# Last four gate tiles chunk by chunk, and the last unit's product, casts and loads rearranged, in a two-layer decoder step

## The chip, the cores and the metric

The kernel runs on one core of one Trainium2 chip. The metric is the device time of one execution in microseconds. Of the kernel before the change three runs are given: 1866.89 us in the median, 1864.61 to 1870.77 us.

## What is computed

One inference step of a decoder trunk of two layers on 1032 rows (1024 of a prompt and 8 samples), 1024 wide, inner width 2048, all in float32. Layer A is an HGRN2 recurrence; layer B is a chunked gated MLP. Behind each mixer comes the per-layer embedding, and at the end a norm. What matters here is the end of layer B:

```python
proj = h @ w_in                      # layer B: u, v, z
u, v, z = jnp.split(proj, 3, axis=-1)
u = jax.nn.gelu(u); v = layernorm(jax.nn.gelu(v), ln_g, ln_b)
s = jnp.einsum('gts,bnsgd->bntgd', w, vc) + b_sp.T[None, None, :, :, None]
y = (u * s * jax.nn.silu(z)) @ w_out
h = h + y
gate = jax.nn.sigmoid(rmsnorm(h, norm_ple[i]) @ w_ple_gate[i])
h = h + gate * (p[i] @ w_ple_proj[i])
return rmsnorm(h, norm_final), ...
```

## The kernel before, in words

**Layout.** Activations lie feature by row: 1032 columns (the rows of the model) in three chunks c0, c1 and c2 of 384, 384 and 264 columns (`CH`, widths `W`, offsets `OFF`), eight tiles of 128 features each. The residual is `hr[c][m]`. A float32 product is made of three TensorE matmuls (`mm3`, lines 228 to 230): both sides are split into a high part, which ScalarE casts, and a low part, which VectorE subtracts (`split`, `split_weights` at lines 149 and 150, `load_list` at 379 and 383), and the matmuls are high by high, high by low, low by high.

**Order.** TensorE's order is written out by hand: a main program, with side programs that are advanced at its ticks. The other engines' orders are made by a scheduler when the kernel is built, by dependencies and priorities (`high_priority`); on the chip each engine runs its own list in order. All the loads and stores around the change are issued by SyncE, in one order, over eight semaphore lanes: a transfer is issued once the one eight before it has landed.

**The last unit of layer B** (g = 7, lines 1580 to 1603). `unit` multiplies two feature tiles by two chunks with seven instead of eight block products, whose sums VectorE forms from the results in PSUM (`u`, `c`); one copy is on ScalarE (`u2`, line 493). In its turns `spatial` makes for each of two tiles and three chunks the product `psp` with the spatial weights (TensorE, 1526), adds the bias (VectorE, 1529), multiplies by u (GpSimd, 1535), and then by the sigmoid and by z (ScalarE 1541, VectorE 1542 and 1543), and stores the rows to `ozd` (1544). Hooks of this unit reload rows of `ozd` that the output projection needs, split them into the operands `xm[..]` and `hh/hl` (`load_zt`, `load_list`), and split p (`p_in_act`, in `first`) for p's products.

**The output projection** (`out_phase`, key "ob"). Its `begin` (1608 to 1626) starts the reload of the rows (2,0), which are chunk 2's first eight tiles (`load_zt(zt, [(2, 0)], ..., 1, 8)`: the first eight loads are issued, the splits follow later in `run(more)`), issues the loads of sums into the `hr` tiles (`load_sums`, line 1320: `h<-d3t`), and makes the second half of p's products (`pple`: `ps_pple` in PSUM, copied by ScalarE at 350 into eight tiles that are free here and, for chunk 2, into `hr[2]`, stored to `ppd` at 351). Behind them stands the first plain product, `ps_o`, for c0, c1 and c2 in turn: c0 reads `bh_12427`, c1 reads `xm[1]` for its first four tiles and `xm[0]` for its last four, c2 reads the rows (2,0), which are `hh[2]/hl[2]` (`bh_12429/bl_12432`). `xm[0]` is `xmh_10550/xml_10551`.

**The gates and the end** (`ple(1, ...)`). Gate tiles m = 0..7 each make 24 matmuls for a chunk, a sigmoid (1273), the product with `pj` (1274), the addition to `hr` (1275) and the squares (263, 264). Tiles 0 and 1, and 6 and 7, go in a pair, chunk by chunk; behind tile 7 of a chunk its final norm (`final`: 279, 282, 237, 290) and its outputs `yt` (1651 on GpSimd, 1653 on VectorE) and their stores (1655) follow.

Of the kernel before, what the change touches and what calls it, by code (L numbers as in the profile page):

```python
# [13 lines left out]
ALU = mybir.AluOpType  # L14
# [66 lines left out]
def trunk_kernel(ctx, tc, xT, st, pT, nrm, wina, lbl, gna, wouta, winb, lng, lnb, lngr, lnbr,  # L81
# [74 lines left out]
    staged = {}  # L156

# [7 lines left out]
    def load(n, wait=False):  # L165
        if n >= len(order) or n in loaded or wait and order[n][0] == "B":
            return
        if order[n][0][0].isupper():
            loaded[n] = load_unit(*order[n])
            return  # L170
        if n not in staged:
            fetch_weights(n)
        stg = staged.pop(n)
        with tc.high_priority(offset=PRI if order[n][:2] == ("p", 1) or order[n][0] in ("b", "g") else 0):
            loaded[n] = split_weights(stg, 1024, PLAIN, wp)
# [216 lines left out]
    def one(tile):  # L392
        return lambda w: tile()[:, :w].rearrange("p (k t) -> p k t", k=1)
# [873 lines left out]
    def ple(l, ep, hh, hl, ssq, done, mid=None):  # L1267
# [15 lines left out]
        def start(m):  # L1283
            pj = ep.tile([P, T], F32, name="pj", bufs=2)
            nc.sync.dma_start(pj, ppd[l][m])
            return take("g", l, m), pj

        def pair(m):
            a, b = start(m), start(m + 1)
            for c in CH:  # L1290
                group(m, c, *a)
                group(m + 1, c, *b)
                if m == KT - 2:
                    done(c)

        pair(0)
        for m in range(2, KT - 2):
            if m == 3 and mid:
                mid()
            a = start(m)  # L1300
            for c in CH:
                group(m, c, *a)
        pair(KT - 2)
# [208 lines left out]
    def spatial(g, vn, us, wt, then={}, early=False):  # L1512
# [8 lines left out]
        def pre(mm, c):  # L1521
# [13 lines left out]
            G.tensor_tensor(s[:, :w], s[:, :w], us[mm, c][:, :w], ALU.mult)  # L1535
# [25 lines left out]
    for g in range(8):  # L1561
# [18 lines left out]
        else:  # L1580
# [9 lines left out]
            zq = load_zt(zt, [(1, 0), (0, 0), (1, 4)],  # L1590
# [3 lines left out]
            def fetch(n):  # L1594
                return lambda: [next(zq, None) for _ in range(n)]

            def first():
                fetch(ZQ)()
                p_in_act(1, lambda w: ws[0].tile([P, 512], F32, name="ssum", bufs=2)[:, :w])

            spatial(g, vn, us, take("B", 2 * MI + 2 * g), {0: first, 1: lambda: next(sums), 2: fetch(4), 3: fetch(8), 4: fetch(4)}, True)
# [5 lines left out]
    def begin(up, raw, rows, load_h):  # L1607
# [10 lines left out]
        more = load_zt(zt, [(2, 0)], one(lambda: next(turns)()), 1, 8)  # L1618
# [11 lines left out]

    with ExitStack() as sE:
# [112 lines left out]
```

## Time and profile before

| what | us |
|---|---|
| median of three runs | 1866.89 (1864.61 to 1870.77) |
| the profiled execution, its own time | 1863.58 |
| its span, first to last instruction | 1861.6 |
| TensorE busy in the span | 1822.4 (98%) |
| VectorE busy | 1360.5 (73%) |
| ScalarE busy | 897.6 (48%) |
| GpSimd busy | 402.3 (22%) |
| granted TensorE clock, mean | 0.995 of full speed |

Times below are microseconds from the start of the span. An instruction's row gives its start, its duration, engine, line, operation, output and inputs with their tile names, and in brackets how long the engine had been idle and what released it. A row that is marked x4 holds four instructions in a run. In a table of windows stand the busy time of each engine and its number of instructions, the clock, the share of the 16 DMA engines and the bytes per second. The last unit runs from about 1545 to 1569, p's products from 1569 to 1583, the first `ps_o` from 1583 to 1594, and the gates fill the last 90 us.

### The profile page before, as it was taken

The numbers are of one execution on the slowest core, as the hardware profiler recorded it, in microseconds if no ns is written. First come the engines' busy times: TensorE is split into PE (matmuls) and PEld (weight loads), VectorE is DVE, ScalarE is ACT, GpSimd is POOL, SyncE is SP. The second block draws the span as 40 slices with busy tenths as digits, with TensorE's granted clock in tenths as the row PEclk, the third lists the DMA queues.
The fourth block names the chain that finished last, engine by engine and source line by source line (L and its number), as shares of the span: only waits on it lengthen the run. The fifth ranks groups of instructions, "written<-read, shape, count | busy, mean of one in ns | idle before, by whom it ended". The sixth has DMA issues, their size and how long they took to land.

```text
span 1861.6 us, 37133 instructions
## 1 busy us (share of the span) xinstructions
PE 1822.4 (98%) x14458; PEld 1788.6 (96%) x14458; DVE 1360.5 (73%) x2760; ACT 897.6 (48%) x1905; POOL 402.3 (22%) x407
## 2 busy tenths in 40 slices
PE   8999999999999999999999999999999999999997
PEld 7999999999999998999999999999999999999997
DVE  7766888889888875867756755577778877877744
ACT  7533366556656655344444544434443435444342
POOL 4000011111111110000323233354444552000222
PEclk9999999999999999999999999999999999999999
DMA  6233344345444355853244343323334546953223
GB/s 220 79 112 106 112 127 128 108 152 182 149 130 140 117 176 185 278 184 96 87 145 140 101 136 92 95 79 119 129 117 143 172 129 215 305 179 104 72 92 114
DMA packets 164560, 258.11 MB, mean 139 GB/s; under 512 B 16096, under 2 KB 136864, under 8 KB 163360
## 3 DMA queue, kind: packets, MB, share of 16 engines
q1 hardware_dynamic: 164384, 255.74, 43.5%
q8 instruction: 113, 1.85, 0.4%
q14 instruction: 63, 0.52, 0.1%
HBM read 182.88 MB, written 72.80 MB: 137 GB/s over the span
## 4 chain that ended last, share of the span: by engine, by line
PE 80%; DVE 10%; DMA 5%; issue 2%; POOL 1%; ACT 1%; SPq 0%; DVEq 0%; ACTq 0%; POOLq 0%
PE ps_proj L228 19%; PE ps_proj L230 18%; PE ps_proj L229 18%; PE ps_d L228 2%; PE ps_o L228 2%; PE ps_d L230 2%; PE ps_d L229 2%; PE ps_o L229 2%; PE ps_o L230 2%; DVE wlo L150 1%; PE psp L1526 1%; DMA vb<-vd 1%; PE pt_o L899 1%; PE pt_g L1408 1%; PE pC L807 1%
## 5 line engine op out<-in xcount | busy, mean ns | idle before, releaser
L228 PE MATMUL ps_proj<-bh,whi 128*128 128x264 f32 (+1 forms) x2248 | 719.2, 320 | 4.3 <-ACT u L493 1.3
L229 PE MATMUL ps_proj<-bl,whi 128*128 128x264 f32 (+1 forms) x2248 | 700.8, 312 | 5.4 <-DVE bl L224 2.7
L230 PE MATMUL ps_proj<-bh,wlo 128*128 128x264 f32 (+1 forms) x2248 | 700.9, 312 | 1.2 <-DVE wlo L150 1.2
L228 PEld LDWEIGHTS ps_proj<-bh,whi 128*128 128x128 f32 x2248 | 423.6, 188 | 12.3 <-issue 3.3
L229 PEld LDWEIGHTS ps_proj<-bl,whi 128*128 128x128 f32 x2248 | 424.1, 189 | 8.9 <-DVE bl L224 5.4
L230 PEld LDWEIGHTS ps_proj<-bh,wlo 128*128 128x128 f32 x2248 | 422.6, 188 | 2.1 <-DVE wlo L150 2.1
L150 DVE TENSOR_TENSOR wlo<-wstg,whi 128x1024 fp32r<-128x1024 f32 x148 | 183.7, 1241 | 109.4 <-ACT whi L149 109.1
L149 ACT CAST whi<-wstg 128x1024 fp32r<-128x1024 f32 x148 | 155.2, 1049 | 150.0 <-PE ps_proj L229 125.0
L149 ACT CAST shi<-ssum 128x512 fp32r<-128x512 f32 x152 | 94.1, 621 | 187.3 <-PE ps_proj L229 90.1
L150 DVE TENSOR_TENSOR slo<-ssum,shi 128x512 fp32r<-128x512 f32 x152 | 113.9, 751 | 9.2 <-ACT shi L149 8.8
L237 POOL TENSOR_TENSOR rsq<-rms_e,mhalf 128x3 f32<-128x3 f32 x15 | 17.8, 1187 | 368.1 <-DVE rms_e L282 368.1
L857 DVE TENSOR_TENSOR qk<-qk,t 128x384 f32<-128x384 f32 (+1 forms) x144 | 77.2, 540 | 12.0 <-PE pC L807 11.3
L228 PE MATMUL ps_proj<-xmh,shi 128*128 128x384 f32 x244 | 83.0, 340 | 1.9 <-ACT xmh L223 1.7
L229 PE MATMUL ps_proj<-xml,shi 128*128 128x384 f32 x244 | 81.9, 336 | 0.7 <-DVE xml L224 0.7
L230 PE MATMUL ps_proj<-xmh,slo 128*128 128x384 f32 x244 | 81.7, 335 | 0.0
L228 PE MATMUL ps_o<-bh,whi 128*128 128x384 f32 (+1 forms) x232 | 73.4, 316 | 0.0
L230 PE MATMUL ps_o<-bh,wlo 128*128 128x384 f32 (+1 forms) x232 | 72.7, 313 | 0.0
L229 PE MATMUL ps_o<-bl,whi 128*128 128x384 f32 (+1 forms) x232 | 72.7, 313 | 0.0
L1535 POOL TENSOR_TENSOR s<-s,u 128x384 f32<-128x384 f32 (+1 forms) x48 | 54.1, 1127 | 70.9 <-DVE s L1529 70.3
L1274 DVE TENSOR_TENSOR tmp<-tmp,pj 128x384 f32<-128x384 f32 (+1 forms) x48 | 25.6, 534 | 55.9 <-ACT tmp L1273 52.0
L237 POOL TENSOR_TENSOR rsq<-ss_e,mhalf 128x3 f32<-128x3 f32 (+2 forms) x32 | 28.4, 889 | 145.7 <-DVE ss_e L893 145.7
L264 POOL TENSOR_TENSOR ssq<-ssq,tmp 128x384 f32<-128x384 f32 (+1 forms) x36 | 34.3, 951 | 108.1 <-ACT tmp L263 108.1
(376 smaller groups left out, 4135.8 us busy)
## 6 DMA issues: line engine op xcount, KB each, us to landing
wstg<-in_wina SPq DMA_DIRECT2D x48, 512.0 KB, 3.8
wstg<-in_winb SPq DMA_DIRECT2D x48, 512.0 KB, 4.0
pj<-ppd SPq DMA_DIRECT2D x16, 516.0 KB, 4.9
S<-in_st SPq DMA_DIRECT2D x16, 512.0 KB, 5.4
vb<-vd SPq DMA_DIRECT2D x16, 512.0 KB, 4.8
out_so_s<-S SPq DMA_DIRECT2D x16, 512.0 KB, 3.5
wstg<-in_wouta SPq DMA_DIRECT2D x16, 512.0 KB, 4.2
wstg<-in_wgate SPq DMA_DIRECT2D x16, 512.0 KB, 3.7
```

The costliest lines, as they stand in the source:

```text
L149: A.copy(hi, src)
L150: V.tensor_tensor(lo, src, hi.bitcast(F32), ALU.subtract)
L228: PE.matmul(ps, wh, xh, start=first, stop=False, skip_group_check=more)
L229: PE.matmul(ps, wh, xl, start=False, stop=False, skip_group_check=more)
L230: PE.matmul(ps, wl, xh, start=False, stop=last, skip_group_check=more)
L237: G.tensor_tensor(y, e, mhalf[:, :n], ALU.pow)
L264: eng.tensor_tensor(ssq, ssq, sq[:, :w], ALU.add)
L807: PE.matmul(out(slice(row, row + kt.shape[1])), kt, qt, start=True, stop=True)
L857: V.tensor_tensor(lev, lev, t2.rearrange("p two (n o) -> p two n o", o=1).broadcast_to([P, 2, n, lv]), ALU.mult)
L899: PE.transpose(pt[:, m, :], on[:, m * P:(m + 1) * P], ident)
L1274: V.tensor_tensor(gt[:, :w], gt[:, :w], pj[:, OFF[c]:OFF[c] + w], ALU.mult)
L1535: G.tensor_tensor(s[:, :w], s[:, :w], us[mm, c][:, :w], ALU.mult)
```

## The change

Four things. **(1)** In layer B the last four gate tiles (4 to 7) go chunk by chunk together, so that c0 of all four comes first, then c1, then c2; `pj` gets four buffers, and the weights of tiles 6 and 7 are split into the room of `xm[0]` and `xm[1]`, which is free by then (`spare`). **(2)** In the last unit the product of s and u is made on VectorE. **(3)** p's rows are loaded and split by `load_list` with a lag of two, at four hooks; each cast stands behind the copy `u2` on ScalarE, each subtraction behind the sum `rest["sum"]` on VectorE. **(4)** The four rows (1,4), which are `xm[0]`, are no longer reloaded in the unit but in `begin`, ahead of the rows (2,0), in the same list with the same lag of eight: the first eight loads are now (1,4) and the first four of (2,0), and the last four of (2,0) are loaded in `run(more)`.

```diff
@@ def load
         stg = staged.pop(n)
         with tc.high_priority(offset=PRI if order[n][:2] == ("p", 1) or order[n][0] in ("b", "g") else 0):
-            loaded[n] = split_weights(stg, 1024, PLAIN, wp)
+            if order[n] in spare:
+                hi, lo = loaded[n] = spare[order[n]]()
+                split(hi, lo, stg)
+            else:
+                loaded[n] = split_weights(stg, 1024, PLAIN, wp)
@@ def ple
-            pj = ep.tile([P, T], F32, name="pj", bufs=2)
+            pj = ep.tile([P, T], F32, name="pj", bufs=4 if l else 2)
             nc.sync.dma_start(pj, ppd[l][m])
             return take("g", l, m), pj
 
-        def pair(m):
-            a, b = start(m), start(m + 1)
+        def several(m, n):
+            a = [start(m)]
             for c in CH:
-                group(m, c, *a)
-                group(m + 1, c, *b)
-                if m == KT - 2:
+                for i in range(n):
+                    if i == len(a):
+                        a.append(start(m + i))
+                    group(m + i, c, *a[i])
+                if m + n == KT:
                     done(c)
 
-        pair(0)
-        for m in range(2, KT - 2):
+        end = 4 if l else 2
+        several(0, 2)
+        for m in range(2, KT - end):
             if m == 3 and mid:
                 mid()
-            a = start(m)
-            for c in CH:
-                group(m, c, *a)
-        pair(KT - 2)
+            several(m, 1)
+        several(KT - end, end)
@@ spatial
-            G.tensor_tensor(s[:, :w], s[:, :w], us[mm, c][:, :w], ALU.mult)
+            (V if g == 7 else G).tensor_tensor(s[:, :w], s[:, :w], us[mm, c][:, :w], ALU.mult)
@@ g == 7
-            zq = load_zt(zt, [(1, 0), (0, 0), (1, 4)],
+            zq = load_zt(zt, [(1, 0), (0, 0)],
                          lambda w: next(zq_to)[:, :w].rearrange("p (k t) -> p k t", k=1),
                          1, ZQ, False)
...
-            def first():
-                fetch(ZQ)()
-                p_in_act(1, lambda w: ws[0].tile([P, 512], F32, name="ssum", bufs=2)[:, :w])
-
-            spatial(g, vn, us, take("B", 2 * MI + 2 * g), {0: first, 1: lambda: next(sums), 2: fetch(4), 3: fetch(8), 4: fetch(4)}, True)
+            pieces = [(pT[1][:, k, OFF[c]:OFF[c] + W[c]], ph[c][:, k, :], pl[c][:, k, :], W[c]) for c in CH for k in range(2)]
+            pq = load_list(pieces, lambda w: ws[0].tile([P, 512], F32, name="ssum", bufs=2)[:, :w], 2, False, True)
+
+            def both(m, n):
+                def go():
+                    for _ in range(m):
+                        next(pq, None)
+                    fetch(n)()
+                return go
+
+            spatial(g, vn, us, take("B", 2 * MI + 2 * g),
+                    {0: both(2, ZQ), 1: lambda: next(sums), 2: both(2, 4), 3: both(2, 8), 4: both(2, 0)}, True)
@@ begin
-        more = load_zt(zt, [(2, 0)], one(lambda: next(turns)()), 1, 8)
+        more = load_zt(zt, [(1, 4), (2, 0)], one(lambda: next(turns)()), 1, 8)
@@ after out_phase
+    for m in range(2):
+        spare["g", 1, KT - 2 + m] = lambda m=m: [t.rearrange("p k t -> p (k t)")[:, :1024] for t in xm[m]]
```

What this does to the engines' lists is seen at three places. Each row is a line of the program, an operation, its output and inputs, and the shape; x4 marks four in a run. Line numbers are 5 or 6 higher in the changed kernel here.

ScalarE around the copy `u2` (`COPY u`) and at the end of the last unit; `bh_12429<-ssum` are p's casts, `sg` the sigmoids of z, `pple_t<-ps_pple` the copies of p's products. Before:

```order
L1541 ACTIVATE sg<-ps_proj 128x264
L379 CAST bh_12427<-bspb 128x384 x2
L379 CAST bh_12427<-gb 128x384
L223 CAST bh_12429<-ssum 128x384
L493 COPY u_19513<-ps_proj 128x384
...
L1541 ACTIVATE sg<-c_19629 128x384
L379 CAST xmh_10550<-wstg_19376 128x384
L1541 ACTIVATE sg<-u_19599 128x384
L149 CAST whi<-wstg 128x1024
L350 COPY pple_t<-ps_pple 128x384
L1541 ACTIVATE sg<-u_19513 128x384
L350 COPY pple_t<-ps_pple 128x384 x7
```

After:

```order
L1547 ACTIVATE sg<-ps_proj 128x264 x2
L384 CAST bh_12427<-bspb 128x384 x2
L384 CAST bh_12427<-gb 128x384
L498 COPY u_19493<-ps_proj 128x384
L384 CAST bh_12429<-ssum 128x384 x2
...
L1547 ACTIVATE sg<-c_19617 128x384
L384 CAST bh_12429<-ssum 128x264 x2
L1547 ACTIVATE sg<-u_19591 128x384
L149 CAST whi<-wstg 128x1024
L1547 ACTIVATE sg<-u_19493 128x384
L355 COPY pple_t<-ps_pple 128x384 x8
```

The copy no longer has p's casts ahead of it; p's casts for chunk 2 now stand between two sigmoids, and both last sigmoids stand ahead of the first copy of p's products, where before one of the copies went between them.

SyncE at `begin`; `zr`, `raw` and `sql` are the tiles into which rows are reloaded, `ozd_75` holds chunk 2, and `h<-d3t` are the loads of sums. Before:

```order
L371 DMA zr<-ozd_75 128x264 x3
...
L351 DMA ppd_4_88<-pple_t 128x384
L371 DMA raw<-ozd_75 128x264 x4
L371 DMA sql<-ozd_75 128x264
L1320 DMA h_0_19693<-d3t_129 128x384
...
L189 DMA wstg<-in_woutb 128x1024
...
L351 DMA ppd_7_91<-h_7_19716 128x264
L1107 DMA h_0_19693<-hd_10556 128x384
```

After:

```order
L376 DMA raw<-ozd_75 128x264 x3
L376 DMA sql<-ozd_75 128x264
L1326 DMA h_0_19681<-d3t_129 128x384
...
L194 DMA wstg<-in_woutb 128x1024
L1326 DMA h_2_19691<-d3t_131 128x384
...
L356 DMA ppd_7_91<-pple_t 128x384
...
L356 DMA ppd_7_91<-h_7_19704 128x264
L376 DMA zr<-ozd_75 128x264 x3
L376 DMA raw<-ozd_75 128x264
L1112 DMA h_0_19681<-hd_10556 128x384
```

All eight rows of (2,0) stood ahead of the sixteen `h<-d3t` and one weight tile; now four of them do, and the other four stand behind the sixteen, the weight tile and ten of the stores to `ppd`.

VectorE at the same place: `bl_12432` are the low parts of (2,0), `xml_10551` those of (1,4), and `ssum` and `slo` belong to the weights of the next unit. Before:

```order
L383 TENSOR_TENSOR bl_12432<-zr,bh_12429 128x264 x3
L383 TENSOR_TENSOR bl_12432<-raw,bh_12429 128x264 x4
L383 TENSOR_TENSOR bl_12432<-sql,bh_12429 128x264
L224 TENSOR_TENSOR bl_12431<-h_0_19693,bh_12428 128x384
```

After:

```order
L229 TENSOR_TENSOR bl_12431<-h_7_19688,bh_12428 128x384
L199 TENSOR_TENSOR ssum<-wstg 128x512
L204 TENSOR_TENSOR ssum<-wstg 128x512
L150 TENSOR_TENSOR slo<-ssum,shi 128x512
L201 TENSOR_TENSOR ssum<-ssum,wstg 128x512
L1128 COPY raw<-h_1_19682 128x384
L150 TENSOR_TENSOR slo<-ssum,shi 128x512
L388 TENSOR_TENSOR bl_12432<-zr,bh_12429 128x264
L150 TENSOR_TENSOR slo<-ssum,shi 128x512
L388 TENSOR_TENSOR bl_12432<-zr,bh_12429 128x264 x2
L388 TENSOR_TENSOR bl_12432<-raw,bh_12429 128x264
```

The last four subtractions of (2,0) stood ahead of every split of the sums `h`; they now stand behind twelve of those splits, three sums and three of the weights' splits. The two buffers of `ssum` are the last two that hold c1's copies of p's products, so the first two sums wait for the stores `ppd<-pple_t` that empty them.

More of the change, by code (lines that the diff above doesn't have):

```diff
@@ L156, in trunk_kernel @@
     staged = {}
+    spare = {}
     def fetch_weights(n):
```

## The prediction

> **What bounds the kernel now.** I read the page's head first, then TensorE's waits in the part that the change touches, then windows, then the rows around each wait.
>
> ```profile
> span 1861.6 us, 37133 instructions
> PE 1822.4 (98%) x14458; PEld 1788.6 (96%) x14458; DVE 1360.5 (73%) x2760; ACT 897.6 (48%) x1905; POOL 402.3 (22%) x407
> ```
>
> TensorE sets the time: 39 us of the span are not its work. A change that leaves the matmuls as they are can win only what TensorE waits, and loses what it makes TensorE wait. The longest waits from 1425 us to the end (in total, times, longest):
>
> ```profile
> PE ps_pple L228 <- ACT pple_t L350: 1.4, 1, 1.4
> PE pss L279 <- ACT sql L257: 1.4, 1, 1.4
> PE pbc L290 <- POOL rsq L237: 1.3, 1, 1.3
> ```
>
> The second and third belong to the final norm behind the last matmul, the first to p's products; two smaller ones (1.13 and 0.88) are in the last unit, and their rows follow below. By windows (PE's busy time comes behind the length):
>
> ```profile
> 1550.00:1560.00 10.00, 9.12 (x56) 8.87 (x55) 8.63 (x19) 4.79 (x11) 1.09 (x1) 1.00 0.81 254
> 1560.00:1570.00 10.00, 8.87 (x56) 8.65 (x56) 9.55 (x16) 6.49 (x14) 2.55 (x3) 1.00 0.54 170
> 1570.00:1580.00 10.00, 8.52 (x49) 7.88 (x48) 7.91 (x14) 5.04 (x11) 1.27 (x1) 1.00 0.65 179
> 1580.00:1590.00 10.00, 10.00 (x66) 10.00 (x66) 4.64 (x10) 6.59 (x16) 0.00 (x0) 1.00 0.96 313
> 1590.00:1600.00 10.00, 10.00 (x67) 10.00 (x66) 7.06 (x13) 5.88 (x11) 0.00 (x0) 1.00 1.03 352
> ```
>
> So 0.88 + 1.13 + 1.48 = 3.5 us are to be had in the unit, and from 1580 to 1600, where the reloads are moved, nothing: TensorE is full there and the DMA engines are at 0.96 to 1.03. That is the place to be careful with.
>
> **The unit: three waits.**
>
> ```profile
> 1554.37 0.51 ACT L223 CAST bh<-ssum 128x384 fp32r<-128x384 f32 x1 [2.71 <-DMA ssum<-in_pT]
> 1554.79 0.47 ACT L493 COPY u<-ps_proj 128x384 f32<-128x384 f32 x1
> 1555.31 0.44 PE L228 MATMUL ps_proj<-bh,whi 128*128 128x384 f32 x1 [0.88 <-ACT u L493]
> 1565.05 1.12 POOL L1535 TENSOR_TENSOR s<-s,u 128x384 f32<-128x384 f32 x1 [4.88 <-DVE s L1529]
> 1565.23 1.36 DVE L383 TENSOR_TENSOR bl<-wstg,bh 128x384 fp32r<-128x384 f32 x1
> 1566.51 0.55 DVE L516 TENSOR_TENSOR c<-ps_d,u 128x384 f32<-128x384 f32 x1
> 1566.98 0.54 DVE L383 TENSOR_TENSOR bl<-rw,bh 128x384 fp32r<-128x384 f32 x1
> 1567.11 0.44 PE L228 MATMUL ps_d<-bh,whi 128*128 128x384 f32 x1 [1.13 <-DVE c L516]
> ```
>
> The first: the copy u2 stood behind a cast of p that had waited 2.71 us for its load. With the cast behind the copy, the wait is gone: -0.88.
>
> The second: TensorE waits for c22 at 1566.51. Just ahead stands a subtraction that took 1.36 us where its like takes 0.54, while GpSimd multiplied s by u beside it (from 1565.05). Two more of VectorE's instructions ran so late in the unit, so the product on GpSimd costs VectorE 3 x 0.82 = 2.5 us. On VectorE six products (four of 384 columns 0.47 apart, as c and the next subtraction start, two of 264) cost about 2.6 us: even. Four subtractions of xm[0] leave the unit (4 x 0.47 = 1.9 us), and the products stand late in VectorE's list, behind the sums. So the sum comes about 2 us earlier than before, where 1.13 are needed: -1.13. The Trainium skill (SBUF — State Buffer, "Who interferes with whom") has the two engines take one shared port for a whole instruction when VectorE reads two inputs from SBUF and GpSimd reads SBUF; the row agrees (GpSimd's end at 1566.17 plus an undisturbed 0.42 gives the observed end). If the slow subtraction had another cause, the 2.5 us would not come back, the second wait would stay, and the total would be 1.1 us higher.
>
> The third: p's products need their PSUM banks copied out.
>
> ```profile
> 1574.47 0.52 ACT L1541 ACTIVATE sg<-u 128x384 f32<-128x384 f32 x1 [1.86 <-DVE u L529]
> 1574.90 1.22 ACT L350 COPY pple_t<-ps_pple 128x384 f32<-128x384 f32 x3
> 1575.41 0.44 PE L228 MATMUL ps_pple<-bh,whi 128*128 128x384 f32 x1 [1.44 <-ACT pple_t L350]
> 1569.32 0.33 PE L228 MATMUL ps_pple<-bh,whi 128*128 128x384 f32 x1
> ssum<-in_pT SPq DMA_DIRECT2D x2, 132.0 KB, 4.1
> ```
>
> Copies and sigmoids share ScalarE. In the changed list no copy stands ahead of the last sigmoid, and that one waits for a sigmoid tile which VectorE frees only behind the splits of p's chunk 2. These rows' loads are issued when p's c1 is split (about 1563.3 and 1564.2 by VectorE's steps), land 3.5 to 4.1 us later, are cast at about 1567.5 and subtracted at 1568; two products and two of 1549 follow (1.9 us), then a sigmoid and a weight cast (1.0). The first copy starts at about 1573.1 and ends at 1573.55. p's products now begin 2.0 us earlier, at 1567.3; three groups of six matmuls, 0.175 apart, fill three banks until 1570.45. So this wait becomes 3.1 us instead of 1.66 (1.44 and a short one of 0.2): +1.4. Together the unit gives -0.88 - 1.13 + 1.4 = -0.6, and the end of p's products, T, goes from 1582.6 to 1582.0. Bounds: -2.0 (the chunk-2 loads land in time, and the third wait is as before) to 0.
>
> **The reloads: the main term.** c2's rows 4 to 7 are needed in the first `ps_o`.
>
> ```profile
> 1582.60 0.34 PE L228 MATMUL ps_o<-bh,whi 128*128 128x384 f32 x1
> 1582.78 0.34 PE L229 MATMUL ps_o<-bl,whi 128*128 128x384 f32 x1
> 1581.87 0.28 PE L228 MATMUL ps_pple<-bh,whi 128*128 128x264 f32 x1
> 1581.99 0.28 PE L229 MATMUL ps_pple<-bl,whi 128*128 128x264 f32 x1
> 1587.87 0.42 DVE L383 TENSOR_TENSOR bl<-sql,bh 128x264 fp32r<-128x264 f32 x1
> ```
>
> c0 and c1 take 48 matmuls x 0.175 = 8.4, each row of c2 3 x 0.12 = 0.36: row 4 is due at T + 9.8, and undisturbed the product ends at T + 11.25 (1593.85). Before, the last low part was done at 1588.3, 4 us in advance. Now the loads of rows 4 to 7 stand behind a weight tile, eleven `h<-d3t` and ten stores, and VectorE's part behind the splits of h and the next weights. The same stretch of the queue before:
>
> ```profile
> 1583.76 1.23 DVE L150 TENSOR_TENSOR wlo<-wstg,whi 128x1024 fp32r<-128x1024 f32 x1 [5.84 <-ACT whi L149]
> 1586.72 0.38 SPq L189 DMA_DIRECT2D wstg<-in_woutb x1
> 1587.14 7.13 SPq L1320 DMA_DIRECT2D h<-d3t x12
> 1594.47 1.37 SPq L351 DMA_DIRECT2D ppd<-pple_t x3
> 1596.04 2.24 SPq L351 DMA_DIRECT2D ppd<-h x4
> 1598.38 0.39 SPq L1107 DMA_DIRECT2D h<-hd x1
> ppd<-pple_t SPq DMA_DIRECT2D x8, 192.0 KB, 4.2
> 1592.00:1594.00 2.00, 2.00 (x18) 2.00 (x17) 1.12 (x2) 1.08 (x3) 0.00 (x0) 1.00 1.05 386
> ```
>
> From 1586.72 to 1598.38 one weight tile (0.52 MB), 15 transfers of 0.197 MB and four of 0.135 were issued: 4.0 MB in 11.7 us, 345 GB/s. In the changed list the weight tile waits for the low part of an earlier one (before: done 2.4 us behind T), so it is issued at T + 2.4 at the earliest, and from there the queue is drained: no eight older transfers are in flight, for which I allow a first landing 1.0 us behind the pure rate. The stores that empty the `ssum` buffers end 3.86 MB into the stretch: at 352 GB/s (the window of 1590 to 1600) 11.0 us, T + 14.4. Then VectorE makes, in this order, two sums, a split, a sum, a copy, a split, the low part of row 4, a split, and three more low parts: five of 512 columns and one more at 0.59 (between 0.47 for 384 and 1.14 for 1024), five short ones at 0.35, 5.3 us: T + 19.7. The loads land earlier (4.93 MB: T + 17.4). Row 7's matmuls end the product at about T + 20.2, against T + 11.25: TensorE waits **9.0 us**. Bounds: at 386 GB/s, the best window quoted, without the extra 1.0 and with VectorE in advance, the loads' landing at T + 15.2 decides, and with a cast, a subtraction and the matmuls the product ends at T + 16.3: 5.0. At 313 GB/s (the window of 1580 to 1590) VectorE begins at T + 15.7: 10.3. A load that is issued earlier on an idle queue does not help, since the list is in order.
>
> Does anything regain it? The stages behind show no wait of TensorE from 1580 to the end of the gates, so they are TensorE's own work and are pushed back as a whole. The rows (1,4) themselves are loaded under p's products and split by about T + 3.5, due at T + 6.3: no cost.
>
> **The gates and the end.**
>
> ```profile
> 1848.40 0.28 PE L230 MATMUL ps_proj<-bh,wlo 128*128 128x264 f32 x1
> 1852.05 5.10 DVE L1653 SCALAR_TENSOR_TENSOR yt<-h,g,pbc 128x384 f32<-128x384 f32 x11
> 1853.12 0.83 PE L290 MATMUL pbc<-ident,rsq 128*128 128x128 f32 x6 [1.28 <-POOL rsq L237]
> 1858.00:1860.00 2.00, 0.00 (x0) 0.00 (x0) 0.00 (x0) 0.00 (x0) 0.00 (x0) 0.50 1.01 352
> ```
>
> 13 us lie between the last matmul and the end. The chain of c2's norm stays: sigmoid, product, addition, squares, two small products, rsq. But of the eleven `yt` from 1852.05 five belong to c1 and the stores saturate the queue; chunk by chunk c1's are out earlier, so c2's six start when `pbc` is there (1854.0), end 0.6 us earlier, and find a free queue: -0.7 (bounds 0 and -1.5). Against it four weight tiles are wanted within four groups of 4.2 us, and the fifth's low part comes just when it is due: +0.3 (0 to +1).
>
> **Sum:** -0.6 + 9.0 - 0.7 + 0.3 = +8.0. The profiled execution took 1863.58 with a span of 1861.6; so a span of 1869.6 and a time of 1871.6. That execution lies 3.3 us below the median of the three; added to the median it is 1874.9. Between the two, nearer the median, I say **1874**.
>
> **Rivals.** (a) *As it says*: rows 4 to 7 are not late, because VectorE and the queue run far ahead of what I think, and all three waits of the unit vanish: -3.5 - 0.7 = -4.2, 1862.7. It decides if row 4's low part is done by T + 9.8. For it speaks that the eight rows were 4 us early before; against, that at T + 2.4 over 3.8 MB stand ahead, which no window moved in 7 us. 10%. (b) *Rows in time, but ScalarE's third wait grows*: -0.6 - 0.7 + 0.3 = -1.0, 1866. 8%. (c) *The queue is late, but at its lower bound*, with the unit's -2.0 and the end's -1.5: +1.5 to +5, around 1870. 15%. (d) *The gates too*: weight tiles 5 to 7 wait behind each other and cost 1 to 4 us on top of the forecast: 1877. 7%; against it, a weight tile lands in 3.7 to 4 us, under the 4.2 of a group. My forecast has 60%: its own range is 1870 to 1878.
>
> What a measurement can tell here is about 0.3%, 5.6 us. Faster by more than that: only (a) with a little luck, 0.06. Within: the rest of (a), (b), (c), and the forecast's lower edge, 0.36. Slower: 0.58. The range that holds 8 of 10 reaches down over (b) and (c): 1865 to 1879.
>
> **What would show it.** One wait of TensorE of some 9 us before a `ps_o` matmul of 264 columns that reads row 4 of c2, put down to a low part of line 388 or to a cast of line 384 behind `zr<-ozd`; `zr<-ozd` issued at about T + 12 to T + 14. No wait for the copy u2 and none for c22; a longer one before the fourth group of `ps_pple`. No instruction of VectorE of 1.36 us in the unit. VectorE's last `yt` in a run of six, not eleven, and the span's end some 12 us behind the last matmul. I am wrong if rows 4 to 7 are split before T + 10, or if stages behind show that TensorE had waits to give back.

## The result: 0.56% slower

The changed kernel took 1876.59 us in the median of eight runs (1875.14 to 1881.45), the kernel before 1866.91 beside it (1861.58 to 1871.06): a ratio of 1.0056 by all the runs (the two medians alone give 1.0052), with a 95% interval of 1.004 to 1.0073, which is 7.5 to 13.6 us. The profiled execution has a span of 1875.5 us.

The two programs are the same up to the last unit, but their profiled executions do not reach it at the same moment: its first `psp` in the trace (the first behind 1540 us) starts at 1542.66 before and at 1543.86 after, and in other executions of this study at up to 1549.6. So everything below is counted from that row to the end of the span, in four stretches. They are worked out from the starts of four rows in each trace: that `psp`, the first `ps_o`, the gates' first and last sigmoid (line 1273, in the changed kernel 1278), and the span. A span is given to 0.1 us, so the last two rows hold to 0.1 us as well.

| stretch | before | after | difference |
|---|---|---|---|
| last unit and p's products: `psp` to first `ps_o` | 39.94 | 39.38 | -0.56 |
| projection: first `ps_o` to first sigmoid of a gate | 181.12 | 194.14 | +13.02 |
| gates: first to last sigmoid | 85.00 | 85.68 | +0.68 |
| end: last sigmoid to end of span | 12.88 | 12.44 | -0.44 |
| together | 318.94 | 331.64 | +12.70 |

The loss is in the projection alone. TensorE's four longest waits in the changed kernel from 1425 us to the end name it (in total, times, longest):

```profile
PE ps_o L233 <- ACT bh L384: 9.3, 1, 9.3
PE ps_pple L233 <- ACT pple_t L355: 2.2, 1, 2.2
PE pss L284 <- ACT sql L262: 1.5, 1, 1.5
PE pbc L295 <- POOL rsq L242: 1.2, 1, 1.2
```

The waits for the copy u2 and for c22 are gone, as meant. A new one of 9.3 us stands before `ps_o`. Around it the timeline of the changed kernel shows the queue, then VectorE, ScalarE and TensorE:

```profile
1585.65 0.33 SPq L194 DMA_DIRECT2D wstg<-in_woutb  x1
1586.03 5.97 SPq L1326 DMA_DIRECT2D h<-d3t  x11
1592.20 3.28 SPq L356 DMA_DIRECT2D ppd<-pple_t  x6
1595.53 2.29 SPq L356 DMA_DIRECT2D ppd<-h  x4
1597.92 1.37 SPq L376 DMA_DIRECT2D zr<-ozd  x3
1598.65 0.69 DVE L199 TENSOR_TENSOR ssum<-wstg 128x512 f32<-128x512 f32 x1 [1.70 <-DMA ppd<-pple_t]
1601.48 0.62 ACT L149 CAST shi<-ssum 128x512 fp32r<-128x512 f32 x1 [1.49 <-DVE ssum L201]
1602.00 0.41 ACT L384 CAST bh<-zr 128x264 fp32r<-128x264 f32 x1
1583.24 0.34 PE L233 MATMUL ps_o<-bh,whi 128*128 128x384 f32 x1
1592.89 0.28 PE L235 MATMUL ps_o<-bh,wlo 128*128 128x264 f32 x1
1602.46 0.59 PE L233 MATMUL ps_o<-bh,whi 128*128 128x264 f32 x1 [9.29 <-ACT bh L384]
```

The first `ps_o` starts at T = 1583.24. c2's fourth row ends TensorE's work at 1593.0, T + 9.8; the loads of the next rows are issued at 1597.92, T + 14.7, behind the weight tile, eleven loads of sums and ten stores, and the first of them lands 3.3 us later. On ScalarE the cast of row 4 stands behind the cast of a sum that waits for VectorE, so it is at 1602.00, 0.8 us behind that landing, and TensorE goes on at 1602.46, T + 19.2.

That is 9.45 us of the 13.0. The rest is in how it goes on:

```profile
1605.65 0.42 PE L234 MATMUL ps_o<-bl,whi 128*128 128x264 f32 x1
1605.87 0.42 PE L235 MATMUL ps_o<-bh,wlo 128*128 128x264 f32 x1
1606.09 0.52 PE L233 MATMUL ps_o<-bh,whi 128*128 128x384 f32 x1
1606.41 0.52 PE L234 MATMUL ps_o<-bl,whi 128*128 128x384 f32 x1
...
1608.86 0.34 PE L233 MATMUL ps_o<-bh,whi 128*128 128x384 f32 x1
1609.04 0.34 PE L234 MATMUL ps_o<-bl,whi 128*128 128x384 f32 x1
```

A matmul of 264 columns starts 0.22 us behind the one ahead, where it was 0.12, and one of 384 columns 0.32 instead of 0.175, until 1608.7. By windows of the changed kernel the granted clock (the number behind the engines) is halved:

```profile
1601.00:1602.00 1.00, 0.00 (x0) 0.00 (x0) 0.71 (x2) 0.52 (x1) 0.00 (x0) 0.50 0.97 281
1607.00:1608.00 1.00, 1.00 (x4) 1.00 (x4) 0.75 (x1) 0.73 (x2) 0.00 (x0) 0.50 1.05 380
1609.00:1610.00 1.00, 1.00 (x8) 1.00 (x7) 0.07 (x1) 0.00 (x0) 0.00 (x0) 1.00 0.56 92
```

c2's last twelve matmuls take 3.63 us (1602.46 to 1606.09) instead of 1.45, and the nine behind them 2.77 instead of 1.57: 2.2 + 1.2 = 3.4 us, of which 2.4 are the clock (12 x 0.10 and 8 x 0.147) and the rest rows that came one by one. 9.45 + 3.4 = 12.8 of the 13.02.

The unit's small net gain hides two larger numbers. p's products start 24.06 us behind the first `psp`, before 26.66: 2.6 us were won. They then take 2.0 us longer:

```profile
1572.50 0.52 ACT L1547 ACTIVATE sg<-u 128x384 f32<-128x384 f32 x1 [3.18 <-DVE s L1549]
1573.45 0.44 PE L233 MATMUL ps_pple<-bh,whi 128*128 128x384 f32 x1 [2.23 <-ACT pple_t L355]
1574.60 0.52 PE L233 MATMUL ps_pple<-bh,whi 128*128 128x384 f32 x1
1574.92 0.52 PE L234 MATMUL ps_pple<-bl,whi 128*128 128x384 f32 x1
1575.00:1576.00 1.00, 1.00 (x5) 1.00 (x4) 0.48 (x2) 0.32 (x1) 0.00 (x0) 0.50 0.83 290
```

The last sigmoid waited 3.18 us for VectorE's product with the sigmoid, p's copies stood behind it, TensorE waited 2.23 us, and then its clock was halved here too, from 1574.6 to 1578.0: ten matmuls of 384 columns at 0.32 us, 1.5 us.

### The profile page after: what moved, and what is told of

Its sections match the earlier page's. It is cut to its first block, busy times and chain, and to the rows that moved or that the text cites. A ratio compares the mean times of both kernels' runs of the same rounds, so it can differ in the third digit from the quotient of the medians.

```text
span 1875.5 us, 37116 instructions
## 1 busy us (share of the span) xinstructions
PE 1826.4 (97%) x14458; PEld 1792.4 (96%) x14458; DVE 1363.1 (73%) x2766; ACT 898.2 (48%) x1905; POOL 396.8 (21%) x401
## 4 chain that ended last, share of the span: by engine, by line
PE 81%; DVE 9%; DMA 5%; issue 2%; POOL 1%; ACT 1%; SPq 1%; DVEq 0%; ACTq 0%; POOLq 0%
PE ps_proj L233 19%; PE ps_proj L234 19%; PE ps_proj L235 19%; PE ps_d L233 3%; PE ps_d L235 2%; PE ps_d L234 2%; PE ps_o L234 2%; PE ps_o L233 2%; PE ps_o L235 2%; PE psp L1532 1%; DVE wlo L150 1%; PE pt_o L904 1%; PE pt_g L1414 1%; PE pC L812 1%; PE po L235 1%
## 5 line engine op out<-in xcount | busy, mean ns | idle before, releaser
L233 PE MATMUL ps_proj<-bh,whi 128*128 128x384 f32 (+1 forms) x2200 | 704.0, 320 | 4.0 <-DVE vl L229 1.9
L234 PE MATMUL ps_proj<-bl,whi 128*128 128x384 f32 (+1 forms) x2200 | 685.8, 312 | 4.3 <-POOL bl L229 2.4
L235 PE MATMUL ps_proj<-bh,wlo 128*128 128x384 f32 (+1 forms) x2200 | 685.9, 312 | 1.2 <-DVE wlo L150 1.2
L233 PEld LDWEIGHTS ps_proj<-bh,whi 128*128 128x128 f32 x2200 | 414.9, 189 | 11.6 <-issue 4.6
L234 PEld LDWEIGHTS ps_proj<-bl,whi 128*128 128x128 f32 x2200 | 415.2, 189 | 7.6 <-DVE bl L229 4.2
L235 PEld LDWEIGHTS ps_proj<-bh,wlo 128*128 128x128 f32 x2200 | 413.7, 188 | 2.1 <-DVE wlo L150 2.1
L1279 DVE TENSOR_TENSOR tmp<-tmp,pj 128x384 f32<-128x384 f32 (+1 forms) x48 | 25.9, 540 | 52.7 <-ACT tmp L1278 49.1
L233 PE MATMUL ps_proj<-bh,shi 128*128 128x384 f32 x164 | 55.9, 341 | 0.0
```

The lines of the kernel that those rows point to most:

```text
L233: PE.matmul(ps, wh, xh, start=first, stop=False, skip_group_check=more)
L234: PE.matmul(ps, wh, xl, start=False, stop=False, skip_group_check=more)
L235: PE.matmul(ps, wl, xh, start=False, stop=last, skip_group_check=more)
L1279: V.tensor_tensor(gt[:, :w], gt[:, :w], pj[:, OFF[c]:OFF[c] + w], ALU.mult)
```

## The experiments

The theory, Q: the place of c2's last four loads in the queue makes the long wait, and the wait makes the half clock. Rivals: D, the crowd of transfers and splits makes the wait wherever the four loads stand; G, the gates carry a part. All runs were timed beside the kernel before; stretches are those of the table above, each from one profile, so a difference of a few tenths of a microsecond between two kernels shows nothing by itself.

| kernel | ratio to before (95%) | unit | projection | gates | end | together |
|---|---|---|---|---|---|---|
| before | 1 | 39.94 | 181.12 | 85.00 | 12.88 | 318.94 |
| the change | 1.0056 (1.004 to 1.0073) | 39.38 | 194.14 | 85.68 | 12.44 | 331.64 |
| e1_rows_back | 1.002 (1.001 to 1.003) | 42.72 | 181.19 | 85.68 | 12.91 | 322.50 |
| e2_rows_alone | 1.0071 (1.0055 to 1.0088) | 39.74 | 193.39 | 84.99 | 13.72 | 331.84 |
| e3_twelve_ahead | 1.001 (1.0 to 1.002) | 36.95 | 181.86 | 85.68 | 13.00 | 317.49 |
| e4_filled | 1.0077 (1.0062 to 1.0092) | 37.55 | 196.87 | 85.68 | 12.40 | 332.50 |
| e4b_filled_longer | one run, 1877.41 us | 37.22 | 193.21 | 85.68 | 12.36 | 328.47 |
| e5_gates_alone | one run, 1865.77 us | 38.84 | 181.57 | 85.68 | 13.02 | 319.11 |
| e7_product_first | 0.9983 (0.9972 to 0.9994) | 35.33 | 181.87 | 85.72 | 13.25 | 316.17 |
| e8_gates_as_before | 0.9981 (0.9969 to 0.9994) | 35.33 | 182.70 | 85.00 | 13.46 | 316.49 |
| e9_rows_back_product_first | 0.9978 (0.9967 to 0.9988) | 36.48 | 180.96 | 85.69 | 13.04 | 316.17 |
| e10_product_on_gpsimd | 0.9985 (0.9967 to 1.0003) | 36.90 | 181.19 | 85.68 | 12.45 | 316.22 |
| e11_p_as_before | 0.9984 (0.9973 to 0.9994) | 36.41 | 181.18 | 85.68 | 12.99 | 316.26 |
| e12_product_alone | 0.9976 (0.9967 to 0.9986) | 36.81 | 180.95 | 85.00 | 13.22 | 315.98 |

(The expectations call the first `psp` in the trace that of c0; it is the same row.)

### The move of the rows, undone

```diff
-            zq = load_zt(zt, [(1, 0), (0, 0)],
+            zq = load_zt(zt, [(1, 0), (0, 0), (1, 4)],
...
-                    {0: both(2, ZQ), 1: lambda: next(sums), 2: both(2, 4), 3: both(2, 8), 4: both(2, 0)}, True)
+                    {0: both(2, ZQ), 1: lambda: next(sums), 2: both(2, 4), 3: both(2, 8), 4: both(2, 4)}, True)
...
-        more = load_zt(zt, [(1, 4), (2, 0)], one(lambda: next(turns)()), 1, 8)
+        more = load_zt(zt, [(2, 0)], one(lambda: next(turns)()), 1, 8)
```

> The changed kernel with the four rows (1,4) reloaded in the last unit again and only the eight rows (2,0) in the projection's list; the other three parts stay. Theory Q (the place of c2's last four loads in SyncE's queue makes the wait, and the half clock behind it comes from the wait): the 9.3 us wait of the first c2 product is gone and no matmul behind it runs at half clock, so the time falls by 9.3 + 2.5 = about 12 us against the changed kernel, to about 1865. The unit gets four subtractions back (1.9 us of VectorE), so its gain against the kernel before may shrink from 2.6 to 1 us. Rival D (the wait comes from the crowd of transfers and splits under p's products, which the casts of p and the longer third wait make too): a wait of 4 us or more stays there, time 1870 or more. Rival G (the gates and the end carry part of the loss): time 1868 or more although the wait is gone.

Measured 1869.23 us (1866.63 before). The wait of `ps_o` is gone and the projection is back at 181.19, so Q holds for the wait and D falls. But the time is not the 1865 of Q: it is the 1868 or more that G named. By the stretches, 2.8 of the 3.6 us that are left against the kernel before lie in the unit, and only 0.7 in the gates. The unit's wait:

```profile
PE ps_pple L233 <- ACT pple_t L355: 4.9, 1, 4.9
```

With the four subtractions back, the wait for p's copies grew from 2.2 to 4.9 us, and the clock was halved behind it. The change without its worst part is still 0.2% slower than the kernel before, mainly for this reason; that the third wait would cost so much was in no theory.

### The move of the rows, alone

```diff
-            zq = load_zt(zt, [(1, 0), (0, 0), (1, 4)],
+            zq = load_zt(zt, [(1, 0), (0, 0)],
...
-            spatial(g, vn, us, take("B", 2 * MI + 2 * g), {0: first, 1: lambda: next(sums), 2: fetch(4), 3: fetch(8), 4: fetch(4)}, True)
+            spatial(g, vn, us, take("B", 2 * MI + 2 * g), {0: first, 1: lambda: next(sums), 2: fetch(4), 3: fetch(8), 4: fetch(0)}, True)
...
-        more = load_zt(zt, [(2, 0)], one(lambda: next(turns)()), 1, 8)
+        more = load_zt(zt, [(1, 4), (2, 0)], one(lambda: next(turns)()), 1, 8)
```

> The kernel before with nothing changed but the reload of the four rows (1,4), which moves into the projection's list ahead of the rows (2,0). Theory Q: the whole loss appears, a wait of 8 to 10 us before the fifth row of c2 and half clock behind it, time 1876 to 1879. Rival D: the wait is under 4 us, because p's casts and the third wait are as before; time under 1872.

Measured 1878.88 us. The kernel before with this one part shows the whole loss. Its two longest waits:

```profile
PE ps_o L228 <- ACT bh L379: 8.9, 1, 8.9
PE ps_pple L228 <- ACT pple_t L350: 2.8, 1, 2.8
```

### Twelve loads ahead

```diff
         turns = itertools.cycle([lambda: up.tile([P, 384], F32, name="zr", bufs=ZR)] * ZR + [raw] * 4 +
-                                [lambda: sp.tile([P, 384], F32, name="sql", bufs=1)])
-        more = load_zt(zt, [(1, 4), (2, 0)], one(lambda: next(turns)()), 1, 8)
-        for _ in range(8):
+                                [lambda: sp.tile([P, 384], F32, name="sql", bufs=1)] + [lambda m=m: hr[2][m] for m in (2, 3, 0, 1)])
+        more = load_zt(zt, [(1, 4), (2, 0)], one(lambda: next(turns)()), 1, 12)
+        for _ in range(12):
             next(more)
```

> The changed kernel with twelve instead of eight reloads issued ahead of the sums: the last four rows of c2 get buffers of their own, tiles of the residual of chunk 2 that are empty then (hr[2][2], [3], [0], [1]). Nothing else is changed; the four rows (1,4) stay where the change put them. Theory Q: c2's wait is gone (their low parts are done by about T + 6), no half clock, time 12 us under the changed kernel, about 1864 to 1865. Rival D: the queue is full anyway (0.94 to 1.06 of the DMA engines), so with twelve rows ahead of them the loads of sums and the stores are late and the wait only moves to a later product; time 1870 or more.

Measured 1867.62 us. The rows (1,4) stay where the change put them, the same bytes go through the same queue, and only the last four loads of c2 go ahead of the sums: the long wait is gone. The same kernel's waits from 1500 us on:

```profile
PE ps_pple L233 <- ACT pple_t L355: 1.4, 1, 1.4
PE ps_d L233 <- DVE c L521: 1.1, 2, 0.6
```

This and the two runs before settle the cause of the wait. They move the four loads in the queue and, with them, their casts and subtractions in the engines' lists; the two are not told apart. The time is about 3 us above what Q gave, and 0.1% above the kernel before, although the stretches of its one profile are together 1.4 us shorter; no row explains that. The projection is 0.74 us longer than before; there TensorE waits 0.5 us for a c22 at 1645.6 (the longer one in the line above lies at 1500 us, ahead of the unit). Whether the splits of (1,4), which VectorE now makes in the projection, cause that wait is not shown: e10 and e11 make them there too, and have no wait there.

### TensorE kept busy through the wait

```diff
                     if k == 3:
                         yield 1
+                        if key == "ob" and c == 2 and not filled:
+                            filled.append(1)
+                            for _ in range(76):
+                                PE.matmul(ps[:, 264:512], blk(wt[0], 0), b["c2"][0][:, 0, :248], start=True, stop=True, skip_group_check=True)
...
             later = []
+            filled = []
```

> The changed kernel with 76 more matmuls (248 columns, into the unused end of c2's own PSUM bank, about 0.113 us each, 8.6 us in all) between c2's fourth and fifth row, so that TensorE works through most of its wait. The result does not depend on them. If idleness lowers the granted clock, as the changed kernel's windows suggest (0.50 from the wait until 1608.6), the clock stays at 1.00 behind the wait, the twelve matmuls of 264 columns are 0.12 apart instead of 0.22 and the next ones 0.175 instead of 0.32: 2.5 us less than the changed kernel, about 1874. If the half clock has another cause (the load of the DMA engines or the copies), nothing is gained, 1876 to 1877.

Measured 1879.37 us. Contrary to the expectation, the extra matmuls, which open sums of their own in c2's bank, do change the kernel's output; its time can be read all the same. It does not answer the question on the clock, for the rows came later than the fill lasted (T + 22.8 instead of T + 19.2; why is open): 4.1 us of the wait were left, and the clock was halved behind them (0.50 from 1603.1 to 1609.9). A longer fill, which adds to the bank instead of opening sums and leaves the output as it was:

```diff
-                            for _ in range(76):
-                                PE.matmul(ps[:, 264:512], blk(wt[0], 0), b["c2"][0][:, 0, :248], start=True, stop=True, skip_group_check=True)
+                            for _ in range(104):
+                                PE.matmul(ps[:, 264:512], blk(wt[0], 0), b["c2"][0][:, 0, :248], start=False, stop=False, skip_group_check=True)
```

> The changed kernel with 104 instead of 76 extra matmuls between c2's fourth and fifth row, about 11.8 us, so that less than 1.5 us of the wait is left idle (the first try left 4.1 us, and the clock still fell). What they add to c2's bank lies behind its 264 columns and is not read. If idleness lowers the clock: the granted clock stays 1.00 from 1590 to 1615, the matmuls of 264 columns behind are 0.12 apart, the next 0.175. If not: 0.22 and 0.32 as in the changed kernel.

```profile
1606.00:1608.00 2.00, 2.00 (x17) 2.00 (x16) 2.00 (x6) 0.00 (x1) 0.00 (x0) 1.00 0.97 262
1606.92 0.28 PE L233 MATMUL ps_o<-bh,whi 128*128 128x264 f32 x1
1607.04 0.28 PE L234 MATMUL ps_o<-bl,whi 128*128 128x264 f32 x1
1607.28 0.34 PE L233 MATMUL ps_o<-bh,whi 128*128 128x384 f32 x1
1607.45 0.34 PE L234 MATMUL ps_o<-bl,whi 128*128 128x384 f32 x1
```

This is one run. With no gap the clock stays at 1.00, and the matmuls are 0.12 and 0.17 apart: the half clock comes from the idleness, not from the transfers or the copies, which are the same. The fill itself ends at 1605.8, T + 21.7, 2.5 us behind the moment at which the changed kernel went on, so the projection is only 0.9 us shorter.

### The gates, alone and undone

Alone: the kernel before with `several` and `spare` of the change (the first two parts of its diff and the last).

> The kernel before with only the last four gate tiles chunk by chunk. Theory N: from first to last sigmoid 85.7 instead of 85.0 us, from the last matmul to the end 12.7 to 13.2 instead of 13.2: between -0.5 and +0.7 in all. Rival E: the end is shorter by 1 us or more.

Undone: the kernel of the next section with `pair` of the kernel before.

> The same as the last one with the gates in the old order (tiles 4 and 5 one by one, 6 and 7 in a pair). Theory N (chunk by chunk only moves c1's norm from behind the last matmul into the stretch that TensorE fills): the gates, first to last sigmoid, take 85.0 instead of 85.7 us, and the end from the last matmul is 0 to 0.5 us longer; the two kernels differ by under 0.5 us, in this one's favour if at all. Rival E (the earlier outputs empty the queue): this one is 0.5 to 1.5 us slower.

In every profile with the new order the gates take 85.68 to 85.72 us, in every one with the old order 84.99 or 85.00. The end takes 12.36 to 13.25 (ten profiles, 12.8 in the mean) with the new one and 12.88, 13.22, 13.46 and 13.72 (13.3) with the old. So chunk by chunk brings c1's last small products out of the end, where TensorE waits anyway, into the stretch that TensorE fills, for 0.7 us, and gets about 0.5 back at the end. In the time nothing of it is seen: 0.9983 with the new order, 0.9981 with the old. E falls, and N holds but for a tenth: in the run alone gates and end together are 0.8 us longer, where N allowed 0.7.

### The product's place in VectorE's list

```diff
-            (V if g == 7 else G).tensor_tensor(s[:, :w], s[:, :w], us[mm, c][:, :w], ALU.mult)
+            with tc.high_priority(offset=PRI if g == 7 else 0):
+                (V if g == 7 else G).tensor_tensor(s[:, :w], s[:, :w], us[mm, c][:, :w], ALU.mult)
```

In the change the sums, the sigmoids and their products have a priority and the product of s and u has none. Three of the latter therefore stood last in VectorE's list, and behind them the products that free the sigmoids' tiles. In e1 that is seen best:

```profile
1574.51 1.02 DVE L388 TENSOR_TENSOR xml<-wstg,xmh 128x384 fp32r<-128x384 f32 x2
1575.44 1.02 DVE L1541 TENSOR_TENSOR s<-s,u 128x384 f32<-128x384 f32 x2
1576.38 1.02 DVE L1549 TENSOR_TENSOR s<-s,sg 128x384 f32<-128x384 f32 x2
1576.97 0.52 ACT L1547 ACTIVATE sg<-u 128x384 f32<-128x384 f32 x1 [3.42 <-DVE s L1549]
```

> The kernel with twelve reloads ahead, and in the last unit the product of s and u gets the same scheduling priority as the work around it (line 1541 inside high_priority). In the kernels before it three of these products and the two products with the sigmoid stood behind all the subtractions in VectorE's list, so that the sigmoid tile came free late and the copies of p's products with it. Theory V (the third wait comes from the place of the products, not from p's late chunk 2): the wait before the fourth group of p's products (1.4 to 4.9 us in the runs so far) falls under 0.5, the stretch from the unit's first spatial product of c0 to the first output product, which was 36.95, falls to about 35.6, and the time to 1864 to 1866, faster than the kernel before by about 0.1%. Rival P (p's chunk 2, whose loads are issued late, holds ScalarE): the wait stays at 1 us or more, time as with twelve ahead (1867.6).

Measured, on top of twelve loads ahead: 1863.83 us against 1867.55, 0.9983 (0.9972 to 0.9994). There is no wait for p's copies any more, and the unit falls from 36.95 to 35.33. So the place of the products made the third wait. p's late chunk 2 did not: here its last subtraction comes even later, 29.3 us behind the first `psp` instead of 25.9.

### Each other part left out once, and one part alone

With the product first, the rows (1,4) were put back into the unit (as in e1):

> The kernel with the four rows (1,4) back in the last unit, and the product of s and u with the priority of its neighbours. It tells whether moving the four rows is worth anything once the third wait is gone. If VectorE's four subtractions (1.9 us) are what the unit has no room for: a wait of 1 us or more for c22 or for the copies comes back, the stretch from the first spatial product of c0 to the first output product is 36.3 or more (35.3 with the rows moved and twelve ahead), time 1865 to 1867. If VectorE has room for them behind the products: 35.3 to 35.6 and a time like that of the version with twelve ahead (1864), and the move was needless.

1862.24 us, 0.9978. A wait of 0.7 us for p's copies is back and the unit is 36.48, but the projection is 0.9 us shorter; 0.6 of that is a wait for c22 at 1637.8 that the version with twelve ahead and the product first has and this one has not, for a reason that no run shows. Together both have 316.2: the move of the rows was needless. Next, the product back on GpSimd (on the version with twelve ahead):

> The version with twelve ahead and the product first, but with the product of s and u on GpSimd as before. If GpSimd's product slows VectorE as the rows of the kernel before showed (1.36 against 0.54 us, three times): three instructions of VectorE of 1.3 us or more in the unit, and TensorE waits 0.3 to 1.2 us for c22; the stretch is 35.6 to 36.5 (35.3 with the product on VectorE). If the product on VectorE costs as much as it frees: no difference, 35.3, time 1864.

```profile
1566.30 1.26 POOL L1542 TENSOR_TENSOR s<-s,u 128x384 f32<-128x384 f32 x1 [1.02 <-DVE s L1535]
1566.61 1.38 DVE L388 TENSOR_TENSOR bl<-wstg,bh 128x384 fp32r<-128x384 f32 x1
```

VectorE's slow instructions are back beside GpSimd's (1.38, 1.38, and a weight's 1.88 instead of 1.23), and a wait of 1.1 us for p's copies; none for c22. The unit is 36.90, longer than either branch gave, but the three stretches behind it make up for that: the time is 1863.32 us, 0.9985, with an interval that just reaches 1. Then p's rows as before (on the version with twelve ahead):

> The version with twelve ahead and the product first, but with p's rows loaded and cast as before, ahead of the copy u2. If the first wait comes from the cast ahead of the copy: TensorE waits 0.8 to 0.9 us for the copy u2 again, the stretch grows by that, to about 36.2. If it comes from VectorE's crowd, there is no such wait and the stretch is 35.3.

The unit is 36.41, but the wait for the copy u2 did not come back: the expectation was wrong. The product on VectorE has moved the list on ScalarE too. All of these end at 316.2 or 316.3 us (with the old order of the gates it was 316.5). Each part could be missed as long as the product had its neighbours' priority, on either engine, so at last the product alone, on the kernel before:

```diff
-            G.tensor_tensor(s[:, :w], s[:, :w], us[mm, c][:, :w], ALU.mult)
+            with tc.high_priority(offset=PRI if g == 7 else 0):
+                (V if g == 7 else G).tensor_tensor(s[:, :w], s[:, :w], us[mm, c][:, :w], ALU.mult)
```

> The kernel before with one thing changed: in the last unit the product of s and u is made on VectorE, with the priority of its neighbours. p's rows, the four rows (1,4) and the gates are as before. In the four versions before, each of the other parts was missing once, and all four took 316.2 us from the unit's first spatial product in the trace to the end (318.9 before). Theory R (the parts overlap, and this one alone is enough): 316.0 to 316.6 from there to the end, no wait of TensorE over 0.8 us in the unit, time 1862 to 1865, as fast as the best. Rival S (at least two parts are needed): one of the three waits of the kernel before stays with 0.8 us or more, 317 to 318 us, time 1865 to 1867.

1862.56 us against 1867.71: 0.9976 (0.9967 to 0.9986), as fast as the best and with none of the other parts. TensorE's waits in its unit:

```profile
PE ps_pple L228 <- ACT pple_t L350: 0.5, 1, 0.5
...
PE ps_d L228 <- DVE c L516: 0.3, 1, 0.3
```

Of the three waits of 0.9, 1.1 and 1.4 us the first is gone, the others are 0.3 and 0.5. In its ScalarE list the copy u2 stands ahead of two of p's casts, and two stand earlier, ahead of a sigmoid: the scheduler did by itself, for the copy, what the third part of the change wrote out. Theory R holds. This edit changes the engine and the priority together. Since the product on GpSimd with the priority (e10) ended at 316.2 us too, the priority alone may be enough; no run has it alone on the kernel before.

## Why the prediction was right, and where it was not

- **The main term.** The mechanism was right, and its size too small. The product was to end at T + 20.2 instead of T + 11.25, 9.0 us late, all of it TensorE's wait, with bounds of 5.0 and 10.3. TensorE waited 9.3 us, but the product ended at T + 22.85, 11.6 us late. The queue's order gave it: the loads went out at T + 14.7, a little behind the T + 12 to T + 14 forecast, VectorE's sums waited for the stores until T + 15.4 (forecast T + 14.4), and the last low part was done at T + 21.6 (forecast T + 19.7). As forecast, the engines' lists held the rows longer than the queue did. The last part of the difference is the half clock.
- **What was left out: the clock.** No term of the sum had TensorE work slower behind a wait. That is 2.4 us in the projection and 1.5 in p's products: 3.9 of the 4.7 us by which the +12.7 us of the profiles exceed the forecast's +8.0. The timed runs show less than the profiles, 7.5 to 13.6 us, and why is open. That 1874 comes so near to 1876.59 is in part luck: it was set between the sum on the profiled execution (1871.6) and the sum on the median (1874.9), and a term was missing.
- **The unit.** -0.6 was forecast and -0.56 measured, which is luck, since the terms err against each other: the first two waits gave -2.6 instead of -2.0, the third grew to 2.2 us and not to 3.1, and 1.5 us of half clock came in. The reason given for the third wait was half right. The sigmoid did wait for VectorE; but what VectorE was late with was the product's place at the end of its list, not p's chunk 2 (e7).
- **c22.** It was put down to GpSimd's slowing of VectorE. The slowing is real: in each of the three cases before and of two in e10 VectorE's slow instruction ends 0.41 or 0.42 us behind GpSimd's product. But that 0.42 is not an undisturbed subtraction of 384 columns, as the prediction reads it; one takes 0.54, and 0.42 is one of 264. And the slowing alone does not make the wait: e2, which only moves the rows (1,4), and e10 both have the product on GpSimd and no wait for c22.
- **Gates and end.** +0.3 and -0.7 were forecast, +0.68 and -0.44 measured. The 0.68 is not late weights, as the prediction had it, but c1's small products of the norm in a full stretch: between the first and the last sigmoid stand 18 matmuls `pbc` instead of 12, and TensorE has no wait there.
- **Nothing regained.** That the stages behind would give nothing back held: the waits from the first `ps_o` to the gates are the same in both kernels but for the new one.

## What to carry to other kernels

An edit that makes room for loads at the head of a list pushes others behind everything that the same queue holds: for each moved load, add up the bytes that now stand ahead of it and divide by the rate that the queue showed there. Price a wait of TensorE of more than about 2 us above its length: in these runs the matmuls behind it ran at half clock for 3.4 to 6.2 us. Where a scheduler orders by priority, an operation that is moved to a busy engine needs the priority of the work around it; here the product on VectorE with that priority was by itself as good as any version with the other three rearrangements, and those added nothing that these runs can tell from noise.

## What was not expected of the hardware

The half clock after an idle TensorE. Idle times in these runs, and the granted clock behind them: 1.36, 1.44, 1.63 and 1.97 us, 1.00; 2.23 us, 0.50 for 3.4 us; 2.78 us (e2), 1.00; 4.08, 4.86, 8.89 and 9.29 us, 0.50. So 2.2 us can be enough and 2.8 can be harmless.

The traces show what makes the difference. In each execution the granted clock changes only at points of one grid of 3.413 us, from 25 us to the end, and the grid lies elsewhere in every execution: in the changed kernel the half clock lasts from 1574.58 to 1577.99 and from 1598.47 to 1608.71, and 1598.47 - 1574.58 is seven steps. By steps of its own grid the changed kernel reads

```profile
1571.17:1574.58 3.41, 1.18 (x7) 1.13 (x7) 3.41 (x7) 1.65 (x4) 0.00 (x0) 1.00 0.34 119
1574.58:1577.99 3.41, 3.41 (x13) 3.41 (x12) 0.90 (x2) 0.96 (x2) 0.00 (x0) 0.50 0.76 178
1591.64:1595.06 3.42, 1.53 (x13) 1.33 (x11) 2.46 (x6) 2.79 (x6) 0.00 (x0) 1.00 1.05 363
1595.06:1598.47 3.41, 0.00 (x0) 0.00 (x0) 1.43 (x3) 0.79 (x2) 0.00 (x0) 1.00 1.07 371
1598.47:1601.88 3.41, 0.00 (x0) 0.00 (x0) 2.95 (x5) 1.02 (x2) 0.00 (x0) 0.50 1.03 305
1601.88:1605.30 3.42, 2.67 (x9) 2.14 (x10) 3.17 (x8) 1.99 (x6) 0.00 (x0) 0.50 0.90 267
1605.30:1608.71 3.41, 3.41 (x14) 3.41 (x14) 2.92 (x5) 1.56 (x2) 0.00 (x0) 0.50 0.91 316
```

and e2 around its 2.78 us

```profile
1572.52:1575.94 3.42, 1.97 (x12) 1.65 (x10) 3.32 (x6) 1.47 (x2) 1.26 (x1) 1.00 0.54 171
1575.94:1579.35 3.41, 2.08 (x12) 2.08 (x13) 2.51 (x4) 2.13 (x5) 0.00 (x0) 1.00 0.71 200
```

The gap of 2.23 us lies within one step, and the next step is at half clock; the gap of 2.78 us is cut by the grid into 1.45 and 1.33, and nothing happens. A step with 1.89 us idle (1591.64) has no effect either, one that is idle throughout (1595.06) has. At half clock a step with 0.75 us idle (1601.88) does not end it, a full one (1605.30) does. So for these gaps what counts is the idle time within one step, with the limit between 1.9 and 2.2 us. This is read from the traces; no run moved a gap against the grid on purpose, and the limit is not the same everywhere: between 216 and 222 us a step with 1.82 us idle had no effect in the profile of the kernel before and halved the clock in that of e3.

The Trainium skill (TensorE: Matmul & The Clock Gate, "What's actually happening") describes a window of about 3.4 us that runs freely, whatever the kernel does. The grid of 3.413 us agrees with it. The Trainium skill (TensorE: Matmul & The Clock Gate, "Why this matters for your kernels") warns of idle gaps over some 3 us. The 2.23 us lie under that limit and halved the clock all the same. In e3, e7 and e12 no gap was left in the unit that is long enough to meet it.
